# A decoder layer on one core: in the recurrence, a chunk's output products grouped by their contracted rows, and its norm in three parts

## The chip, the cores and the metric

The kernel runs on one core of one Trainium2 chip. A core has five engines that work side by side: PE (TensorE, matrix products), DVE (VectorE), ACT (ScalarE), POOL (GpSimd) and SP (SyncE, which here only issues transfers). Transfers between the chip's memory (HBM) and the core's memory (SBUF) are done by 16 DMA engines. PE writes its results into PSUM, eight banks of 128 partitions by 512 float32 values, from which DVE or ACT reads them.

The metric is the device time of one launch in microseconds. A profile is taken of one execution: it records when each instruction ran on each engine, which clock PE was granted, and what the transfers did. Its span is a little shorter than the time of that execution.

## What is computed

The reference is one decoder layer on 512 tokens of width 1024: a mixer block (an RWKV-7 recurrence beside a dilated attention, joined by gates) and then a PEER block (product-key experts). What matters here is the recurrence with its norm, for 16 heads of 64 channels:

```python
def step(state, inp):
    r_t, w_t, k_t, v_t, a_t, b_t = inp
    sa = jnp.einsum('bhij,bhj->bhi', state, a_t)
    state = (state * w_t[:, :, None, :] + sa[..., None] * b_t[:, :, None, :]
             + v_t[..., None] * k_t[:, :, None, :])
    return state, jnp.einsum('bhij,bhj->bhi', state, r_t)
...
y = wkv7_scan(r_h, hv(decay), k_h, v_h, -kk, kk * a_h)
mu = jnp.mean(y, axis=-1, keepdims=True)
var = jnp.mean(jnp.square(y - mu), axis=-1, keepdims=True)
y = (y - mu) * lax.rsqrt(var + RWKV_GN_EPS) * lnx_g.reshape(H, N) + lnx_b.reshape(H, N)
y = y + jnp.sum(r_h * k_h * r_k, axis=-1, keepdims=True) * v_h
return y.reshape(B, S, RWKV_WIDTH).astype(z.dtype) * g
```

The kernel doesn't take the 512 steps one by one. It cuts the sequence into NC = 8 chunks of C = 64 tokens, solves each chunk's own triangular system beforehand, and then hands a state of 64 x 64 values per head from chunk to chunk.

## The kernel before

`Kern.main` runs four phases one after the other: `phase_mod_n1` (modulation and the normed input n1), `phase_mix` (recurrence and attention), `phase_merge` and `phase_peer`. Large products are made by `gemm_ch`: it loads a weight tile of 512 KB (`wraw`, L124), splits it into a high part on ACT (`whi`, L127) and a low part on DVE (`wlo`, L128), and sums 24 products in one bank of PSUM (`ps_mm`, L141 to L143).

The order of the instructions on each engine is not that of the code. A planner (`schedule_with_timeline_sim`) lays them out along a timeline of its own, by priority and by what is ready; it also sets the waits between engines. The code's order gives the priority, and `first` raises that of the recurrence by AHEAD = 1500. On each engine the instructions then run in the order so fixed.

`attention` weaves two generators: `rw_chain`, three steps for each of the eight chunks, and `both()`, which makes the attention (`at_prep`, `at_core`, `at_end`) and between them gate columns by `gate_cols` (L403 and L404 store them). The gemms, transposes and softmax steps of attention thus fill PE between the steps of the recurrence.

A chunk c in `rw_chain` (L681 to L743), with the heads laid out as p = 0 to 7 and h = 0, 1 (h is the half of the 128 partitions):

- It loads `uv`, `ar`, `bks` and `mr` (512 KB each) from `pt_d` on SP: L694 to L700, in the trace `cuv`, `car`, `cbk` and `cmr`. The first three have two buffers, `cmr` has one.
- First step, for c > 0: `w0` (L705, in the trace `w`), 16 products of `ar` with the state `st`; then `w0s` on DVE (L708), two instructions.
- Second step: `up` (L715), 16 products with the solved system `tt`; its two halves are copied into `uv` by DVE (L716) and ACT (L717). Then one `next(norm, None)`, the first part of the norm of the chunk before.
- Third step: `sp` (L723), 16 products for the new state, added and scaled on DVE (L727, L728; L730 for c = 0); then `yp`, the chunk's output. For each of the 16 (p, h) there are two products into the same 64 x 64 place of one bank: the own one (L733), `mr` with `uv`, over all 128 rows, and the state's (L735), `ar` with `st`, over the 64 rows of half h. ACT copies `yp` to `ys` (L737).

`rw_norm` (L745 to L771) makes the norm of a chunk from `ys`. Its first part loads `bg` (`bgl`, one buffer, L749), and makes mean and difference on DVE (L751 to L753), the square on ACT (L755, tile `sqn`), the variance on DVE (L757, L758), its power -1/2 on POOL (L759) and the scaling on DVE (L760). Its second part turns the chunk by 16 products into `yt` (L766), multiplies it on DVE (L768, tile `yr`, which shares the one buffer of `sqn`), adds on POOL (L769) and stores to `yr_d` from SP (L770).

Before the change the generator of chunk c is made at the end of the chunk's loop body, its first part runs in chunk c+1's second step, and the second part when the loop comes to the end of chunk c+1's body (`run(norm)`, L741).

`yp` and `yt` both have tag "d", for which PSUM has one bank; `w0`, `up` and `sp` share tag "c", also one bank. After the eight chunks `phase_mix` reads `yr_d` back (`yrt`, L356) and splits it (L357, L358) for the gemms of `phase_merge`.

Of the kernel before, what the change touches and what calls it, by code (L numbers as in the profile page):

```python
# [77 lines left out]
def run(gen):  # L78
    for _ in gen:
        pass  # L80
# [20 lines left out]
class Kern:  # L101
# [579 lines left out]
    def rw_chain(self):  # L681

        nc, kp = self.nc, self.kp
        A = (slice(0, 64), slice(64, 128))
        PH = [(p, h) for p in range(8) for h in range(2)]
        st = None
        norm = iter(())
        def chain_ps(tag, name):
            return self.psum.tile([P, 8, C], F32, tag=tag, name=name, bufs=BANKS[tag])

        for c in range(NC):
            pt = self.pt_d[c]
            uv = kp.tile([P, 8, 128], F32, tag="cuv", name="cuv", bufs=2)
            nc.sync.dma_start(uv, pt[:, 3])  # L694
            ar = kp.tile([P, 8, 128], F32, tag="car", name="car", bufs=2)
            nc.sync.dma_start(ar, pt[:, 0])
            bks = kp.tile([P, 8, 128], F32, tag="cbk", name="cbk", bufs=2)
            nc.sync.dma_start(bks, pt[:, 2])
            mr = kp.tile([P, 8, 128], F32, tag="cmr", name="cmr")
            nc.sync.dma_start(mr, pt[:, 1])  # L700
            U = (slice(64, 128), slice(0, 64))
            if c:
                w0 = chain_ps("c", "w0")
                for p, h in PH:
                    nc.tensor.matmul(w0[A[h], p], ar[A[h], p, 0:64], st[A[h], p], start=True, stop=True)  # L705
                w0s = kp.tile([P, 8, C], F32, tag="w0s", name="w0s")
                for h in range(2):
                    nc.vector.tensor_tensor(w0s[A[h]], w0[A[h]], uv[A[h], :, U[h]], op=OP.add)  # L708
                ws = lambda p, h: w0s[A[h], p]
            else:  # L710
                ws = lambda p, h: uv[A[h], p, U[h]]
            yield
            up = chain_ps("c", "up")
            for p, h in PH:
                nc.tensor.matmul(up[A[h], p], self.tt[p // 4][A[h], (p % 4) * 8 + c, :], ws(p, h), start=True, stop=True)  # L715
            nc.vector.tensor_copy(uv[A[0], :, U[0]], up[A[0]])  # L716
            nc.scalar.activation(uv[A[1], :, U[1]], up[A[1]], AF.Copy)  # L717
            next(norm, None)
            yield
            if c < NC - 1:  # L720
                sp = chain_ps("c", "sp")
                for p, h in PH:
                    nc.tensor.matmul(sp[A[h], p], bks[:, p, h * 64:h * 64 + 64], uv[:, p, U[h]], start=True, stop=True)  # L723
                sn = kp.tile([P, 8, C], F32, tag="st", name="st", bufs=2)
                pc = self.pend[:, :, c:c + 1].to_broadcast([P, 8, C])
                if c:
                    nc.vector.tensor_tensor(sn, sp, st, op=OP.add)  # L727
                    nc.vector.tensor_tensor(sn, sn, pc, op=OP.mult)  # L728
                else:
                    nc.vector.tensor_tensor(sn, sp, pc, op=OP.mult)  # L730
            yp = chain_ps("d", "yp")
            for p, h in PH:
                nc.tensor.matmul(yp[A[h], p], mr[:, p, h * 64:h * 64 + 64], uv[:, p, U[h]], start=True, stop=not c)  # L733
                if c:
                    nc.tensor.matmul(yp[A[h], p], ar[A[h], p, 64:128], st[A[h], p], start=False, stop=True)  # L735
            ys = kp.tile([P, 8, C], F32, tag="ys", name="ys", bufs=3)
            nc.scalar.activation(ys, yp, AF.Copy)  # L737
            if c < NC - 1:
                st = sn
            yield  # L740
            run(norm)  # L741
            norm = self.rw_norm(c, ys)
        run(norm)  # L743

    def rw_norm(self, c, ys):  # L745

        nc, kp = self.nc, self.kp
        bg = kp.tile([P, 2, 8, C], F32, tag="bgl", name="bgl")
        nc.sync.dma_start(bg, self.bg_d[c])  # L749
        mean = kp.tile([P, 8], F32, tag="mean", name="mean", bufs=2)  # L750
        nc.vector.tensor_reduce(mean, ys, axis=AX.X, op=OP.add)  # L751
        nc.vector.tensor_scalar(mean, mean, 1.0 / 64, None, op0=OP.mult)
        nc.vector.tensor_tensor(ys, ys, mean[:, :, None].to_broadcast([P, 8, C]), op=OP.subtract)  # L753
        sq = kp.tile([P, 8, C], F32, tag="sqn", name="sqn")
        nc.scalar.activation(sq, ys, AF.Square)  # L755
        var = kp.tile([P, 8], F32, tag="var", name="var", bufs=2)
        nc.vector.tensor_reduce(var, sq, axis=AX.X, op=OP.add)  # L757
        nc.vector.tensor_scalar(var, var, 1.0 / 64, GN_EPS, op0=OP.mult, op1=OP.add)  # L758
        nc.gpsimd.tensor_tensor(var, var, self.hneg.to_broadcast([P, 8]), op=OP.pow)  # L759
        nc.vector.tensor_tensor(ys, ys, var[:, :, None].to_broadcast([P, 8, C]), op=OP.mult)  # L760
        yield

        yt = self.psum.tile([P, 8, C], F32, tag="d", name="yt", bufs=BANKS["d"])
        for p in range(8):
            for a in HALF:
                nc.tensor.matmul(yt[a, p], ys[a, p], self.ident[a, a], start=True, stop=True)  # L766
        yr = kp.tile([P, 8, C], F32, tag="sqn", name="yr")
        nc.vector.tensor_tensor(yr, yt, bg[:, 0], op=OP.mult)  # L768
        nc.gpsimd.tensor_tensor(yr, yr, bg[:, 1], op=OP.add)  # L769
        nc.sync.dma_start(self.yr_d[c], yr)  # L770
        yield  # L771
# [567 lines left out]
```

## Time and profile before

| | us |
|---|---|
| median of 3 runs | 2126.97 |
| lowest and highest | 2125.58 and 2130.1 |
| the profiled execution | 2125.92 |
| its span | 2124.1 |

Mean granted clock of PE over the profiled execution: 0.962 of full speed.

The profile's page gives, for each engine, the busy time in us, its share of the span and the number of instructions. Its slices cut the span into 40 equal parts; a digit is the busy share or the granted clock in tenths (9 is 90% or more). In the lists by line, a row names line, engine, operation, result and operands with their sizes; "x224" is a count, and three numbers with slashes are the shortest, median and longest duration in ns. In the timeline a row begins with its start and duration in us; rows that follow each other with the same text are merged with a count, and what stands in brackets is the engine's idle time before it and what ended it. A row of the list of waits names who waited for whom, then the total in us, the number of times and the longest.

PE shows twice: PEld is the loading of the stationary operand, PE the product itself. Products are pipelined: one may start before the one before it has ended, so the pace is read from start to start. "128\*64 128x64" is 128 contracted rows by 64 output columns of the stationary operand, and a moving operand of 64 columns.

### The profile page before, as it was taken

Reading aid. Unit: us, or ns where it says so; the run is one execution under the profiler, and the core shown is the slowest. Engines: PE = TensorE matmul, PEld = TensorE weight load, DVE = VectorE, ACT = ScalarE, POOL = GpSimd, SP = SyncE. Lnnn points to the kernel's source line nnn. Section 1 sums busy time; section 2 is a strip of 40 time slices with the busy share of each in tenths; the row PEclk is TensorE's granted clock in tenths of the full one; section 3 lists DMA queues with packets and bytes.
Section 4 is the critical chain, followed back from the end, with each engine's and each line's share of the span. In section 5 each row is a group of like instructions: output and inputs, shape, how many; then the busy total and the mean of one; then the engine's idle time right before and its main releaser. Section 6 shows DMA issues by size and latency. Waiting matters only on the chain.

```text
span 2124.1 us, 34025 instructions
## 1 busy us (share of the span) xinstructions
PE 2022.2 (95%) x12529; PEld 1744.0 (82%) x12529; DVE 1600.9 (75%) x3192; ACT 935.8 (44%) x1452; POOL 642.8 (30%) x511
## 2 busy tenths in 40 slices
PE   5999899999999998999999999999959999999999
PEld 4677667877877786899998999999958887877887
DVE  7466894853534555899999999987768898988555
ACT  3756665543324443334334454456633333333332
POOL 2424550221402111001674545420015555551000
PEclk9999989998889998999999999999979999999999
DMA  6666855354435532335998999985589999999763
GB/s 260 224 189 201 256 170 149 94 189 147 140 121 173 186 127 72 108 119 173 386 360 293 334 359 349 375 316 203 198 292 358 388 392 398 394 391 344 230 211 110
DMA packets 236299, 519.45 MB, mean 245 GB/s; under 512 B 35554, under 2 KB 129506, under 8 KB 233572
## 3 DMA queue, kind: packets, MB, share of 16 engines
q1 hardware_dynamic: 180260, 334.27, 46.4%
q0 software_dynamic: 36864, 134.23, 16.9%
q10 hardware_dynamic: 19008, 48.77, 6.0%
q8 instruction: 99, 1.62, 0.3%
q14 instruction: 68, 0.56, 0.1%
HBM read 432.23 MB, written 84.97 MB: 243 GB/s over the span
## 4 chain that ended last, share of the span: by engine, by line
PE 65%; DVE 16%; DMA 10%; issue 4%; ACT 3%; POOL 2%; SPq 0%; DVEq 0%; ACTq 0%; POOLq 0%
PE ps_mm L141 13%; PE ps_mm L143 13%; PE ps_mm L142 13%; DVE wlo L128 4%; PE gps L1132 4%; DMA wraw<-in_v 3%; DMA act<-act_d 2%; DVE row L1150 2%; PE yp L735 2%; PE yp L733 2%; PE ps_a L143 1%; PE ps_a L142 1%; PE ps_a L141 1%; DMA wada<-in_wada 1%; DVE acc L1164 1%
## 5 line engine op out<-in xcount | busy, mean ns | idle before, releaser
L127 ACT ACTIVATE whi<-wraw 128x1024 fp32r<-128x1024 f32 x356 | 370.1, 1042 | 388.6 <-PE ps_mm L142 226.9
L128 DVE TENSOR_TENSOR wlo<-wraw,whi 128x1024 fp32r<-128x1024 f32 x356 | 430.4, 1212 | 131.5 <-ACT whi L127 127.8
L141 PE MATMUL ps_mm<-n2h,whi 128*128 128x384 f32 (+1 forms) x1152 | 399.9, 347 | 3.2 <-ACT act L1203 3.2
L142 PE MATMUL ps_mm<-n2l,whi 128*128 128x384 f32 (+1 forms) x1152 | 398.2, 346 | 0.0
L143 PE MATMUL ps_mm<-n2h,wlo 128*128 128x384 f32 (+1 forms) x1152 | 396.1, 345 | 2.1 <-DVE wlo L128 2.1
L1141 POOL DMA_INDIRECT row<-in_v,xi x128 | 196.7, 1537 | 339.7 <-DVE acc L1164 166.5
L1141 POOL DMA_INDIRECT row<-in_u,xi x128 | 187.0, 1461 | 171.3 <-DVE dots L1150 132.7
L141 PEld LDWEIGHTS ps_mm<-n2h,whi 128*128 128x128 f32 x1152 | 218.4, 190 | 9.1 <-ACT act L1203 4.4
L143 PEld LDWEIGHTS ps_mm<-n2h,wlo 128*128 128x128 f32 x1152 | 218.2, 190 | 7.7 <-DVE wlo L128 2.8
L142 PEld LDWEIGHTS ps_mm<-n2l,whi 128*128 128x128 f32 x1152 | 218.3, 190 | 4.7
L141 PE MATMUL ps_mm<-n1h,whi 128*128 128x512 f32 x464 | 193.8, 421 | 8.8 <-ACT n1h L271 5.0
L143 PE MATMUL ps_mm<-n1h,wlo 128*128 128x512 f32 x464 | 192.5, 415 | 1.2 <-DVE wlo L128 1.2
L142 PE MATMUL ps_mm<-n1l,whi 128*128 128x512 f32 x464 | 192.4, 415 | 0.2 <-DVE n1l L272 0.2
L1250 ACT ACTIVATE wh<-act 128x384 fp32r<-128x384 f32 x128 | 66.9, 525 | 279.1 <-DVE act L1244 144.4
L1164 DVE SCALAR_TENSOR_TENSOR acc<-row,g,acc 128x1024 f32<-128x1024 f32 x127 | 162.3, 1278 | 0.8
L1150 DVE CUSTOM_DVE_ANT_0 row<-row,n2t 128x1024 f32<-128x1024 f32 x128 | 153.0, 1218 | 0.0
L1244 DVE TENSOR_TENSOR act<-act,G 128x384 f32<-128x384 f32 x128 | 69.8, 553 | 87.1 <-DMA act<-act_d 72.6
L1133 ACT ACTIVATE Gs<-gps 128x512 f32<-128x512 f32 x96 | 107.1, 1120 | 57.8 <-PE gps L1132 55.8
L141 PE MATMUL ps_mm<-whi,wh 128*128 128x512 f32 x256 | 92.6, 395 | 29.2 <-ACT wh L1250 29.0
L141 PEld LDWEIGHTS ps_mm<-n1h,whi 128*128 128x128 f32 x464 | 91.1, 198 | 32.5 <-ACT n1h L271 5.0
L143 PEld LDWEIGHTS ps_mm<-n1h,wlo 128*128 128x128 f32 x464 | 91.5, 197 | 23.0 <-DVE wlo L128 2.2
L142 PEld LDWEIGHTS ps_mm<-n1l,whi 128*128 128x128 f32 x464 | 92.1, 198 | 21.7 <-issue 2.4
(405 smaller groups left out, 4000.6 us busy)
## 6 DMA issues: line engine op xcount, KB each, us to landing
wraw<-in_uT SPq DMA_DIRECT2D x128, 512.0 KB
wraw<-in_v SPq DMA_DIRECT2D x128, 512.0 KB
wraw<-in_win SPq DMA_DIRECT2D x60, 512.0 KB
g_d<-Gs ACTq DMA_DIRECT2D x12, 2048.0 KB
G<-g_d SPq DMA_DIRECT2D x16, 1536.0 KB
act_d<-act ACTq DMA_DIRECT2D x120, 192.0 KB
act<-act_d SPq DMA_DIRECT2D x120, 192.0 KB
wada<-in_wada SPq DMA_DIRECT2D x64, 256.0 KB
```

The costliest lines, as they stand in the source:

```text
L127: nc.scalar.activation(hi[:, :n], raw[:, :n], AF.Copy)
L128: nc.vector.tensor_tensor(lo[:, :n], raw[:, :n], hi[:, :n].bitcast(F32), op=OP.subtract)
L141: mm(acc, lh, rh, start=start, stop=False)
L142: mm(acc, lh, rl, start=False, stop=False)
L143: mm(acc, ll, rh, start=False, stop=stop)
L1132: nc.tensor.matmul(g[:, j], E[:, j], A[:, j], start=True, stop=True)
L1133: nc.scalar.activation(Gs[:, :, o:o + 4].rearrange("p i t -> p t i"), g, AF.Copy)
L1141: self.nc.gpsimd.indirect_dma_start(row, None, self.I[tab], bass.IndirectOffsetOnAxis(ap=self.xi[:, n:n + 1], axis=0))
L1150: self.gathered(self.rowp, n, "u", lambda row: nc.vector.tensor_tensor_reduce(out=row, in0=row, in1=self.n2t, scale=1.0, scalar=0.0, op0=O ...
L1164: nc.vector.scalar_tensor_tensor(acc, row, self.gates0[:, n:n + 1], acc, op0=OP.mult, op1=OP.add)
L1244: nc.vector.tensor_tensor(act.rearrange("p (b t) -> p b t", t=GB), act.rearrange("p (b t) -> p b t", t=GB), G[:, :, n % GI, :], op=OP.mult)
L1250: nc.scalar.activation(wh, act, AF.Copy)
```

## The change

Three things are edited, all in `rw_chain` and `rw_norm`:

- The 32 output products of a chunk are issued in two groups: first the 16 of the state (64 contracted rows each), then the 16 own ones (128 rows). The mark `start`, which makes a product overwrite instead of add, is set on the first product of the bank alone (for each half h), no longer on the first product of each of the 16 places.
- `rw_norm` yields once more, after the square, so that it has three parts.
- The parts run at other places: the first (load of `bgl`, mean, difference, square) at the end of the chunk's own third step; the second (variance, power, scaling) in the next chunk's first step, behind `w0s`; the third (`yt`, `yr`, store) in the next chunk's second step, behind the copies of `up`.

```diff
@@ -706,6 +706,7 @@
                 w0s = kp.tile([P, 8, C], F32, tag="w0s", name="w0s")
                 for h in range(2):
                     nc.vector.tensor_tensor(w0s[A[h]], w0[A[h]], uv[A[h], :, U[h]], op=OP.add)
+                next(norm, None)
                 ws = lambda p, h: w0s[A[h], p]
             else:
                 ws = lambda p, h: uv[A[h], p, U[h]]
@@ -715,7 +716,7 @@
                 nc.tensor.matmul(up[A[h], p], self.tt[p // 4][A[h], (p % 4) * 8 + c, :], ws(p, h), start=True, stop=True)
             nc.vector.tensor_copy(uv[A[0], :, U[0]], up[A[0]])
             nc.scalar.activation(uv[A[1], :, U[1]], up[A[1]], AF.Copy)
-            next(norm, None)
+            run(norm)
             yield
             if c < NC - 1:
                 sp = chain_ps("c", "sp")
@@ -728,18 +729,21 @@
                     nc.vector.tensor_tensor(sn, sn, pc, op=OP.mult)
                 else:
                     nc.vector.tensor_tensor(sn, sp, pc, op=OP.mult)
+
             yp = chain_ps("d", "yp")
+            if c:
+                for p, h in PH:
+                    nc.tensor.matmul(yp[A[h], p], ar[A[h], p, 64:128], st[A[h], p], start=p == 0, stop=False)
             for p, h in PH:
-                nc.tensor.matmul(yp[A[h], p], mr[:, p, h * 64:h * 64 + 64], uv[:, p, U[h]], start=True, stop=not c)
-                if c:
-                    nc.tensor.matmul(yp[A[h], p], ar[A[h], p, 64:128], st[A[h], p], start=False, stop=True)
+                nc.tensor.matmul(yp[A[h], p], mr[:, p, h * 64:h * 64 + 64], uv[:, p, U[h]],
+                                 start=not c and p == 0, stop=p == 7)
             ys = kp.tile([P, 8, C], F32, tag="ys", name="ys", bufs=3)
             nc.scalar.activation(ys, yp, AF.Copy)
             if c < NC - 1:
                 st = sn
+            norm = self.rw_norm(c, ys)
+            next(norm)
             yield
-            run(norm)
-            norm = self.rw_norm(c, ys)
         run(norm)
 
     def rw_norm(self, c, ys):
@@ -753,6 +757,7 @@
         nc.vector.tensor_tensor(ys, ys, mean[:, :, None].to_broadcast([P, 8, C]), op=OP.subtract)
         sq = kp.tile([P, 8, C], F32, tag="sqn", name="sqn")
         nc.scalar.activation(sq, ys, AF.Square)
+        yield
         var = kp.tile([P, 8], F32, tag="var", name="var", bufs=2)
         nc.vector.tensor_reduce(var, sq, axis=AX.X, op=OP.add)
         nc.vector.tensor_scalar(var, var, 1.0 / 64, GN_EPS, op0=OP.mult, op1=OP.add)
```

## The prediction

> **What bounds the kernel now.** I read the page first: its busy times, then the granted clock in its 40 slices (one slice is 53.1 us).
>
> ```profile
> PE 2022.2 (95%) x12529; PEld 1744.0 (82%) x12529; DVE 1600.9 (75%) x3192; ACT 935.8 (44%) x1452; POOL 642.8 (30%) x511
> PEclk9999989998889998999999999999979999999999
> ```
>
> PE is busy for 95% of the span. The recurrence lies in slices 9 to 13, where the granted clock falls to 8. So I asked for the stretches of that stage and of those before and after it (busy us of PE, PEld, DVE, ACT, POOL, then granted clock, DMA share and GB/s).
>
> ```profile
> 100.00:300.00 200.00, 181.90 (x1265) 139.60 (x1264) 153.89 (x239) 125.22 (x232) 94.40 (x65) 0.90 0.72 216
> 300.00:440.00 140.00, 138.10 (x1347) 110.01 (x1347) 96.35 (x185) 84.44 (x170) 32.73 (x36) 1.00 0.43 131
> 440.00:672.00 232.00, 232.00 (x2154) 183.09 (x2156) 96.99 (x166) 77.35 (x194) 44.27 (x46) 0.86 0.42 139
> 672.00:700.00 28.00, 24.15 (x126) 18.66 (x124) 16.23 (x25) 15.78 (x27) 6.63 (x5) 0.94 0.83 287
> ```
>
> From 440 to 672 us PE has no idle time at all; DVE is busy for 42% of it, ACT for 33%, DMA for 42%. Whatever PE time goes here shortens the stage, as long as nothing else comes to the front. Next I looked at what PE does there, in the timeline of chunk 1 (start, duration, engine, line, operation, count).
>
> ```profile
> 468.54 0.39 PE L141 MATMUL ps_mm<-n1h,whi 128*128 128x512 f32 x1
> 468.86 0.33 PE L733 MATMUL yp<-cuv,cmr 128*64 128x64 f32 x2
> 469.12 0.33 PE L735 MATMUL yp<-st,car 64*64 64x64 f32 x2
> 469.37 1.15 PE L723 MATMUL sp<-cuv,cbk 128*64 128x64 f32 x32
> 470.36 0.28 PE L733 MATMUL yp<-cuv,cmr 128*64 128x64 f32 x2
> 470.57 0.33 PE L735 MATMUL yp<-st,car 64*64 64x64 f32 x2
> 470.83 0.33 PE L733 MATMUL yp<-cuv,cmr 128*64 128x64 f32 x2
> ...
> 479.35 0.47 PE L733 MATMUL yp<-cuv,cmr 128*64 128x64 f32 x2
> 479.76 0.47 PE L735 MATMUL yp<-st,car 64*64 64x64 f32 x2
> 480.16 1.11 PE L886 MATMUL ps_a<-ident,sc 128*128 128x128 f32 x4
> ```
>
> Every product of 64 columns shows as two passes. Where 16 products of one shape follow each other (sp, L723), 32 passes take about 1 us, 34 ns a pass from start to start. In yp, where L733 (128 contracted rows) and L735 (64 rows) alternate, two passes take 0.26 us at first (470.57 to 470.83) and 0.40 us at the end (479.35 to 479.76, 479.76 to 480.16). The step of 0.26 us holds 0.07 us of passes; about 0.19 us is spent at each change of the contracted rows. How much PE time that is in all, I took from a table of the seven stretches with yp's instructions alone (chunk 1 first, the sum last):
>
> ```profile
> 468.80:480.20 11.40, 10.42 (x64) 0.74 0.25 92
> sum 79.90, PE 69.68; mean PE 9.95
> ```
>
> So 64 passes of yp hold PE for 10.0 us a chunk, 69.7 us in chunks 1 to 7.
>
> **The change, part by part.**
>
> *Grouping the products.* The nearest rows of the new order are in chunk 0, where no state exists and nothing alternates, and in w (L705), which multiplies the same 64 rows of the state that L735 does:
>
> ```profile
> 452.86 1.15 PE L723 MATMUL sp<-cuv,cbk 128*64 128x64 f32 x32
> 453.84 0.99 PE L733 MATMUL yp<-cuv,cmr 128*64 128x64 f32 x28
> 455.34 1.15 PE L705 MATMUL w<-st,car 64*64 64x64 f32 x32
> 456.42 0.68 PE L894 MATMUL ps_a<-vt,ptr 128*64 128x64 f32 x14
> ```
>
> w's 32 passes hold PE from 455.34 to 456.42, 1.08 us; chunk 0's own products run at the same pace (28 in 0.99). Per later chunk the new yp is 1.08 us of state, 1.08 us of own products and one change between them, 0.2 us: 2.4 us, 17 us in seven chunks. Bounds: 2.16 us with no price for the change; 5.2 us if the planner cuts the groups some 16 times by other work (16 x 0.19 us = 3 us). I take 2.4, because the rows of w, up and sp stand in one piece. Gain: 69.7 - 17 = 53 us.
>
> One sum per bank (start on the first product only) adds and removes no instruction; nothing for it, since the gemm lines L141 to L143 add up in one bank at the pace of their neighbours. Bounds from below and above: the 34 ns of a pass, either way, 1 us in all.
>
> *The granted clock.* Behind each of the seven stretches there is a piece at half clock; first and last of seven, and their sum:
>
> ```profile
> 480.20:484.50 4.30, 4.30 (x61) 3.85 (x61) 1.55 (x3) 1.19 (x2) 0.00 (x0) 0.50 0.77 263
> 653.50:658.60 5.10, 5.10 (x31) 4.04 (x32) 2.38 (x6) 1.55 (x3) 0.00 (x0) 0.50 0.09 27
> sum 32.20, PE 32.20 PEld 27.50 DVE 13.97 ACT 11.64 POOL 0.61; mean PE 4.60 PEld 3.93 DVE 2.00 ACT 1.66 POOL 0.09
> 481.61 1.86 PE L705 MATMUL w<-st,car 64*64 64x64 f32 x29
> ```
>
> The same products of w take 1.86 us for 29 passes there and 1.15 us for 32 at full clock: 64 ns a pass against 36, a factor of 1.8. Without the slow clock these 32.2 us of work are 18, a gain of 14 us. It falls away only if the alternation causes the drop. For that speaks that in chunk 1 the drop begins inside the yp stretch (the step of two passes grows there from 0.26 to 0.40 us), that all seven pieces stand right behind one, and that 300 to 440 us, without yp, has 1.00; sp of chunk 0 and w behind it, grouped, run at 34 ns a pass. Bounds: nothing, or 15 us. I take 14.
>
> The Trainium skill, "TensorE: Matmul & The Clock Gate", Part 1 (The HAM clock gate), says that a busy TensorE is granted the full clock and that it drops to half after an idle window of about 3.4 us. By that rule alone the stretches, busy without a gap in the rows, would not drop, and their cause would have to be another, which stays; the sum by it would be 2077. The trace differs here: 0.74 granted in a stretch that is full of matmuls.
>
> *The norm in three parts.* It issues the same instructions in other places. Its first part (the load of bgl, mean, subtraction, square) goes from the next chunk's second step to the end of its own; variance to scaling goes behind w0s; the transposition yt and yr, which stood a chunk later still, go behind the copies of up, ahead of this chunk's sp and yp. On SP the load of bgl now stands ahead of the next chunk's loads of cuv, car, cbk and cmr. Its one buffer is free when POOL's L769 has added yr(c-1), which now comes before yp(c), so SP should not stand longer at it than before, and the weight loads (wraw) behind it neither. The loads of a chunk reuse buffers in a stage whose DMA share is 0.42 and would be 0.59 in the shortened one (0.42 x 232 / 165), below the 0.72 of 100 to 300 us. I take nothing; if SP did stand, PE would lack weights, at most the idle time bounded below. On DVE and ACT the work is the same, 97 and 77 us, in 165 us instead of 232: 59% and 47%, less than in 300 to 440 us (69% and 60%). On POOL 44 us in 165. One wait goes:
>
> ```profile
> ACT sqn L755 <- DMA yr_d<-yr: 9.4, 5, 2.4
> ACT ys L737 <- PE yp L735: 70.9, 7, 11.2
> ```
>
> The square shares its buffer with yr of the chunk before, whose store now leaves before yp; ACT's 9.4 us of standing may go. ACT is off the path: nothing.
>
> What gets a new wait is PE: yt and yp share the one bank of tag "d". Until now yp(c) came ahead of yt(c-1); now yp(c)'s first product waits until DVE has read yt(c-1) (L768), and behind it in PE's order stand yp itself and the gemms and transposes of attention. The chain that must be over by then, as durations:
>
> ```profile
> L753 DVE TENSOR_TENSOR ys<-ys,mean x8: 682/692/694, 456.5 to 655.0; 128x512 f32<-128x512 f32 x8
> L755 ACT ACTIVATE sqn<-ys x8: 620/632/634, 457.3 to 666.3; 128x512 f32<-128x512 f32 x8
> L759 POOL TENSOR_TENSOR var<-var,hneg x8: 1627/1645/2550, 459.6 to 667.9; 128x8 f32<-128x8 f32 x8
> 461.27 0.69 DVE L760 TENSOR_TENSOR ys<-ys,var 128x512 f32<-128x512 f32 x1 [1.81 <-POOL var L759]
> L768 DVE TENSOR_TENSOR yr<-yt,bgl x8: 691/691/694, 485.0 to 673.1; 128x512 f32<-128x512 f32 x8
> ```
>
> In chunk 0 the scaling ends at 461.96, 7.1 us behind the end of yp (454.83, 453.84 + 0.99); with yt (32 passes, 1.1) and yr (0.7) it makes 8.9 us. From one yp to the next PE will have 165 / 8, or 20 us, so this chain has about 9 us to spare. I take nothing, and as upper bound all 8.9 us a chunk.
>
> *What is late next.* Today PE's 10 us in yp hide every lateness of the other engines. With that cover gone, the recurrence itself (w, w0s, up, copies, sp, st) must fit into 20 us a chunk. Its DVE steps:
>
> ```profile
> 457.15 1.39 DVE L708 TENSOR_TENSOR w0s<-w,cuv 64x512 f32<-64x512 f32 x2
> 463.71 0.68 DVE L716 COPY cuv<-up 64x512 f32<-64x512 f32 x1 [0.61 <-PE up L715]
> 470.57 0.69 DVE L727 TENSOR_TENSOR st<-sp,st 128x512 f32<-128x512 f32 x1 [0.37 <-PE sp L723]
> 471.30 0.69 DVE L728 TENSOR_TENSOR st<-st,pend 128x512 f32<-128x512 f32 x1
> ```
>
> That is, at 1.08 us for each of three groups and 0.7 us for each of five DVE steps it is 7 us of work; I allow 10 with handovers (an estimate). Bounds for PE's new idle time: none, or the 9% that 100 to 300 us shows (18.1 of 200 us), 15 us of 165. The nearest row is 300 to 440 us, attention's gemms without yp: 1.9 of 140 us, 1.4%. That is 2 us; I take 4, because the recurrence makes PE wait at more places. In the tail (672 to 700, PE idle for 3.9 us) yr of the last chunk may come earlier; bounds 0 and 4 us gained, I take nothing, since attention's end stands there too.
>
> *Sum.* -53 - 14 + 4 = -63 us. The profiled execution took 2125.9 us (span 2124.1), 1.1 us below the median of 2127.0: 2125.9 - 63 = **2063 us**.
>
> **The rivals.**
>
> - *Other engines come to the front*: PE idle as in 100 to 300 us, 15 us. 2125.9 - 67 + 15 = 2074, up to 2080 if the idling costs clock as it does there (0.90). For it: the cover of 10 us a chunk goes. Against: DVE and ACT stay below their shares of 300 to 440 us, where PE is at 99%.
> - *The half clock stays*: it comes from something else than the alternation. Only the 53 us go, less 4: 2125.9 - 53 + 4 = 2077. For it: PE shows no idle time before the drops. Against: chunk 0. This is where the clock page's rule would put the time.
> - *The groups are cut*: the planner orders by its own timeline and already puts the first products of yp ahead of sp. If it sets other work, or own between state products, and half of the changes stay, half of 67 us goes: 2093.
> - *Slower*: PE stands in front of yp(c) until yr(c-1) has emptied bank "d". If none of the 8.9 us is covered, that is 62 us in seven chunks, and so long a stand may cost the 14 us of clock: 2125.9 - 53 + 62 = 2135. It decides from 53 / 7 = 7.6 us of standing a chunk. Against: other PE work lies before yp in its order, in chunk 1 the gemms between w and sp, some 11 us (up to 468.86):
>
> ```profile
> 457.44 0.48 PE L141 MATMUL ps_mm<-n1h,whi 128*128 128x512 f32 x1
> ```
>
> - *Nothing comes of it*: the price lies in adding a second product to a sum, not in the change of rows. Then 2126. Against: L141 to L143 add 24 times without such a price.
>
> **How the numbers follow.** Forecast 0.68; other engines 0.13; half clock stays 0.08; groups cut 0.06; slower 0.02; nothing 0.02; 0.01 for the rest, faster. Below the forecast: full gain 53 + 15 + 1, no idle time, 4 us of tail: 2053, and 3 us, chosen without a row, for a planner that orders the later program otherwise: 2050. Above: the cases of 2074 to 2080, and half clock with idle time, both losses together (53 us gained, 13 lost): 2086. Range 2050 to 2086. About 0.2% (4 us) is what a measurement of this kernel can tell from no change: faster by more 0.95, within 0.02, slower 0.03.
>
> **What would show it.** Right: the state's products stand as about 32 passes in a piece, the own ones too; yp holds PE for 2 to 3 us a chunk; the stage is some 63 us shorter and its granted clock near 1.00; ACT's wait for yp (10 us a chunk) is gone. Wrong: PE idle in the stage with DVE yr L768 or DVE st L727 as releaser (other engines, or bank "d"); pieces at 0.50 behind yp (clock); yp in pieces of two passes (cut). The time fails below if PE's idle time elsewhere shrinks, above if later stages give back what this one gains.

## The result, and the profile after

| | before | after |
|---|---|---|
| median of 4 runs | 2128.53 us | 2071.46 us |
| lowest and highest | 2125.58 and 2132.05 | 2069.71 and 2073.24 |
| profiled execution (span) | 2125.92 (2124.1) | 2073.24 (2071.4) |

After over before: 0.973, 95% interval 0.9717 to 0.9742. The changed kernel is 57 us faster; 2063 was forecast, from 2050 to 2086.

First the page of the changed kernel, its row of PE and its row of the granted clock.

```profile
PE 1959.7 (95%) x12529; PEld 1699.5 (82%) x12529; DVE 1606.0 (78%) x3192; ACT 938.4 (45%) x1454; POOL 639.8 (31%) x511
PEclk9999989999999989999999999999979999999999
```

PE runs the same 12529 instructions in 62.5 us less, and the run of digits 8 over the recurrence is gone. To see where the time went, the stage is cut alike in both kernels: from the first product of `up` (L715; L716 after) to DVE's first multiplication of a gate in the merge phase (L950; L955 after). Columns: window, its length, busy us of PE, PEld, DVE, ACT, POOL, granted clock, DMA share, GB/s. The view by windows, before:

```profile
444.00:712.10 268.10, 263.67 (x2303) 208.02 (x2303) 115.48 (x193) 97.67 (x228) 46.90 (x45) 0.87 0.46 151
```

and after, the stage as a whole and four pieces of 40 us of it:

```profile
443.90:652.90 209.00, 201.06 (x2304) 164.60 (x2304) 118.02 (x193) 100.17 (x230) 45.09 (x45) 0.98 0.58 198
440.00:480.00 40.00, 40.00 (x532) 33.13 (x530) 22.20 (x38) 17.15 (x41) 9.79 (x14) 1.00 0.67 230
480.00:520.00 40.00, 40.00 (x565) 33.17 (x560) 25.62 (x44) 21.14 (x48) 9.72 (x7) 1.00 0.59 198
520.00:560.00 40.00, 38.79 (x518) 31.96 (x517) 28.86 (x50) 16.46 (x46) 17.30 (x22) 1.00 0.61 204
560.00:600.00 40.00, 40.00 (x481) 32.52 (x480) 19.03 (x33) 17.38 (x48) 5.85 (x4) 1.00 0.43 147
```

The stage is 59.1 us shorter. PE is busy for 62.6 us less (263.67 to 201.06) and idle for 3.5 us more (268.10 - 263.67 = 4.4 before, 7.9 after). From 440 to 600 us PE is still all but full (158.79 of 160 us), now at a clock of 1.00.

How much of it yp is, from the same window of the view for yp's instructions alone; before, and then after:

```profile
460.00:660.00 200.00, 69.70 (x448) 0.84 0.40 128
```

```profile
460.00:660.00 200.00, 17.56 (x448) 0.97 0.59 202
```

The same 448 passes hold PE for 52.1 us less. What that looks like in chunk 1 and in chunk 4 shows the timeline of PE after (start, duration):

```profile
468.57 1.15 PE L724 MATMUL sp<-cuv,cbk 128*64 128x64 f32 x32
469.66 1.15 PE L736 MATMUL yp<-st,car 64*64 64x64 f32 x32
470.74 1.15 PE L738 MATMUL yp<-cuv,cmr 128*64 128x64 f32 x32
471.82 0.33 PE L891 MATMUL ps_a<-ident,sc 128*128 128x128 f32 x1
...
546.60 0.80 PE L738 MATMUL yp<-cuv,cmr 128*64 128x64 f32 x18
547.52 0.45 PE L705 MATMUL w<-st,car 64*64 64x64 f32 x8
547.90 0.33 PE L738 MATMUL yp<-cuv,cmr 128*64 128x64 f32 x2
548.16 0.32 PE L705 MATMUL w<-st,car 64*64 64x64 f32 x2
548.41 0.33 PE L738 MATMUL yp<-cuv,cmr 128*64 128x64 f32 x2
```

In chunk 1 each group stands as 32 passes in a piece, 1.08 us from start to start. In chunk 4 the planner lays the next chunk's `w` (64 rows) between yp's own products (128 rows), and the old step of 0.26 us for two passes is back. `w` goes into another bank than yp (tag "c", not "d"), so the step isn't the price of adding twice to one place.

PE's longest wait stands at the end of the stage. Its own waits in the whole stage, and then the chain of waits from 600 to 640 us (start, duration), both after:

```profile
PE ps_a L938 <- DVE ya L932: 5.4, 1, 5.4
PE w L705 <- issue: 1.1, 1, 1.1
PE ps_a L891 <- ACT sc L884: 1.0, 1, 1.0
```

```profile
614.48 5.12 DMA o_d<-ot
619.66 5.96 DMA oall<-o_d
...
627.43 4.63 DVE oall L930 x4
632.06 1.74 DVE ya L932 x2
633.85 1.54 PE ps_a L938 x6
```

No wait of PE for bank "d" is among them. The longest is attention's end: the store of its last block, the load of `oall`, and DVE's combination hold L938 until 633 us, and PE has run out of other work. The stage had idle time at its end before the change too: none from 440 to 672 us, so all of its 4.4 us behind that.

### The profile page after: what moved, and what is told of

It is laid out like the page before. It is cut to its first block, busy times and chain, and to the rows that moved or that the text cites. A ratio compares the mean times of both kernels' runs of the same rounds, so it can differ in the third digit from the quotient of the medians.

```text
span 2071.4 us, 34017 instructions
## 1 busy us (share of the span) xinstructions
PE 1959.7 (95%) x12529; PEld 1699.5 (82%) x12529; DVE 1606.0 (78%) x3192; ACT 938.4 (45%) x1454; POOL 639.8 (31%) x511
## 4 chain that ended last, share of the span: by engine, by line
PE 62%; DVE 17%; DMA 11%; issue 5%; ACT 3%; POOL 2%; SPq 0%; DVEq 0%; ACTq 0%; POOLq 0%
PE ps_mm L141 14%; PE ps_mm L143 13%; PE ps_mm L142 13%; DMA act<-act_d 4%; PE gps L1137 4%; DVE wlo L128 4%; DVE row L1155 2%; DMA wada<-in_wada 2%; PE ps_a L143 2%; PE ps_a L141 2%; PE ps_a L142 2%; DMA wraw<-in_v 2%; DVE acc L1169 1%; DMA G<-g_d 1%; POOL acc L443 1%
```

## The experiments

The twelve runs, of eleven variants and of the changed kernel once more, came in four groups, each beside runs of the kernel before on the same chip; medians of the kernel before were 2128.5, 2128.7, 2126.7 and 2128.5 us there.

**Grouping alone, norm in its old two parts at its old places.** The diff against the kernel before:

```diff
+            if c:
+                for p, h in PH:
+                    nc.tensor.matmul(yp[A[h], p], ar[A[h], p, 64:128], st[A[h], p], start=p == 0, stop=False)
             for p, h in PH:
-                nc.tensor.matmul(yp[A[h], p], mr[:, p, h * 64:h * 64 + 64], uv[:, p, U[h]], start=True, stop=not c)
-                if c:
-                    nc.tensor.matmul(yp[A[h], p], ar[A[h], p, 64:128], st[A[h], p], start=False, stop=True)
+                nc.tensor.matmul(yp[A[h], p], mr[:, p, h * 64:h * 64 + 64], uv[:, p, U[h]],
+                                 start=not c and p == 0, stop=p == 7)
```

> The products grouped (one sum per bank), the norm in two parts at its old places. Theory: the price lay in the changes between 128 and 64 contracted rows, so the grouping alone brings the gain: yp holds PE for some 17 us in chunks 1 to 7 instead of 69.7, no half clock behind it, time 2066 to 2080. Rival: the new places of the norm are needed for the gain (yr of the last chunk and the stores of yr earlier), then 2085 or more.

Measured: 2066.07 us (2063.71 to 2067.56), ratio 0.9708 (0.9681 to 0.9736); from 460 to 660 us yp holds PE for 18.23 us. The grouping brings 62 us, more than the whole change; its highest run lies below the lowest of the changed kernel.

**The norm's move alone**, the products alternating as before. The diff is that of the change without the lines of yp.

> The norm in three parts at its new places, the products alternating as before. Theory: yp still holds PE for about 69 us, PE stays without idle time in the stage, time 2122 to 2133, the same as before. Rival (the norm's places matter by themselves): 2115 or less.

Measured: 2132.70 us, ratio 1.002 (1.0001 to 1.0039): 4 us slower than before, by an interval that only just leaves out no change. In the profiled executions the stage is 5.6 us longer (273.7 and 268.1 us).

**One sum per bank alone**: the two products alternate as before, but `start` stands on the first product of the bank only.

```diff
-  mr[:, p, h * 64:h * 64 + 64], uv[:, p, U[h]], start=True, stop=not c)
+  mr[:, p, h * 64:h * 64 + 64], uv[:, p, U[h]], start=p == 0, stop=not c and p == 7)
...
-  ar[A[h], p, 64:128], st[A[h], p], start=False, stop=True)
+  ar[A[h], p, 64:128], st[A[h], p], start=False, stop=p == 7)
```

> As before, with the products alternating, but one sum per bank: the mark that makes a product overwrite stands on the first product of each half alone. Theory (changes of contracted rows): nothing moves, two passes still take 0.26 us at full clock, time 2124 to 2133. Rival (the price lies in opening and adding to 16 sums in one bank): yp falls to a few us a chunk and the time to 2070 to 2080.

Measured: 2129.68 us, ratio 1.0004 (0.9989 to 1.0018). The marks cost nothing and bring nothing. With the grouping's 62 us this also rules out that the price was in adding a second product, for the grouped kernel adds the same 16.

**Groups of two**: the changed kernel, with the state's products of p for both h and then the own ones of p, so that the rows change half as often as before the change.

```diff
+            for p in range(8):
+                if c:
+                    for h in range(2):
+                        nc.tensor.matmul(yp[A[h], p], ar[A[h], p, 64:128], st[A[h], p], start=p == 0, stop=False)
+                for h in range(2):
+                    nc.tensor.matmul(yp[A[h], p], mr[:, p, h * 64:h * 64 + 64], uv[:, p, U[h]],
+                                     start=not c and p == 0, stop=p == 7)
```

> The changed kernel, but with the products in groups of two instead of 16: two of the state, two own ones, and so on, which makes 15 changes of rows inside a chunk's yp instead of 1 (31 with alternation). Theory: at 0.19 us a change plus 64 passes of 34 ns yp takes 5.1 us a chunk, 19 us more in seven chunks than grouped by 16: about 2090. If stretches of 5 us also bring the half clock back, up to 14 us more: 2104. Rival (the price is per second product in a place, not per change): 2128.

Measured: 2081.45 us, ratio 0.9787 (0.9751 to 0.9823). The timeline of this kernel's PE in chunk 1:

```profile
475.68 0.33 PE L737 MATMUL yp<-st,car 64*64 64x64 f32 x4
475.94 0.34 PE L739 MATMUL yp<-cuv,cmr 128*64 128x64 f32 x4
476.21 0.33 PE L737 MATMUL yp<-st,car 64*64 64x64 f32 x4
476.47 0.34 PE L739 MATMUL yp<-cuv,cmr 128*64 128x64 f32 x4
```

A step of four passes takes 0.263 us, hardly more than the 0.257 us that the alternation needs for two. So a chunk's yp takes half of its time at full clock, 16 x 0.263 = 4.2 us, and the time stays below the 2090 us that I had expected from 0.19 us a change. And the clock stays full, in these windows of the same kernel:

```profile
480.00:520.00 40.00, 40.00 (x515) 31.88 (x515) 22.22 (x34) 16.82 (x40) 5.85 (x4) 1.00 0.60 189
560.00:600.00 40.00, 40.00 (x468) 32.39 (x468) 17.79 (x28) 13.75 (x33) 4.71 (x4) 1.00 0.59 185
```

The steps from the state's products to the own ones of the same place, and from those to the state's of the next place, take the same 0.26 us: the price goes with the change of rows, not with adding to the place just written.

After this group the question was why the changed kernel is 5 us behind the grouping alone.

**Four buffers for attention's output tile**, once in the changed kernel and once in the kernel with the grouping alone:

```diff
-  ax.tile([P, OW], F32, tag="ot", name="ot", bufs=2)
+  ax.tile([P, OW], F32, tag="ot", name="ot", bufs=4)
```

> The changed kernel with four buffers instead of two for attention's output tile ot. Theory A (the 5 us that the changed kernel is behind the kernel with the grouping alone lie in its tail: attention's last blocks stand at the store of ot, 4.6 us of DVE's waiting in two places, and attention's end comes late): 2067 to 2069 us. Rival B (they lie in the places of the norm, yt ahead of yp above all): 2071 us, as before, within 0.1%.

> The kernel before with the grouping alone and four buffers for ot. Theory A (store of ot in the tail): 2062 to 2064 us, 2 to 4 below the grouping alone (2066.1). Rival B: 2066 us.

Measured: 2068.89 us in the changed kernel, ratio 0.9725 (0.9706 to 0.9745). That is what theory A gave, but the interval overlaps that of the changed kernel. With the grouping alone 2060.38 us, 0.9687 (0.9667 to 0.9707), the lowest median of all; the interval overlaps that of the grouping alone. In the profiled executions the stage gets shorter by about the same in both, 209.0 to 203.2 us and 205.1 to 199.8. The waits that the buffers remove are these of the changed kernel, in DVE's timeline of attention's last four blocks (in brackets the idle time before and its releaser):

```profile
579.51 0.69 DVE L882 TENSOR_REDUCE ot<-sc 128x4 f32<-128x512 f32 x1
585.80 0.69 DVE L882 TENSOR_REDUCE ot<-sc 128x4 f32<-128x512 f32 x1
595.75 0.69 DVE L882 TENSOR_REDUCE ot<-sc 128x4 f32<-128x512 f32 x1 [2.02 <-DMA o_d<-ot]
604.02 0.69 DVE L882 TENSOR_REDUCE ot<-sc 128x4 f32<-128x512 f32 x1 [2.54 <-DMA o_d<-ot]
```

The kernel with the grouping alone shows no such wait and gains as much, so these waits are not all that the buffers change.

**Own products first**, then the state's, in the changed kernel; the two loops of yp change places.

> The changed kernel with the 16 own products ahead of the 16 of the state. In the changed kernel's chunk 4 the planner alternates the next chunk's w (64 rows) with the own products of yp (128 rows), 4.17 us in place of 2.23. With the own ones first, w can only meet the state's products, which have the same rows. Theory (each change of rows costs about 0.15 to 0.19 us): no stretch of yp above 2.5 us, and 2069 us, 2 to 3 us below the changed kernel. Rival (the planner puts it elsewhere, or the time given back is lost in the tail): 2071 us.

Measured: 2066.46 us, ratio 0.9713 (0.9692 to 0.9734): 5 us below the changed kernel, where 2 to 3 were expected. In the profiled executions the stage is 2.7 us shorter, as expected (206.3 and 209.0 us); the rest doesn't show there. In chunk 4 the planner still mixes w into yp, now as 64 rows among 64 rows, and in the timeline of this kernel's PE nothing is left of the step of 0.26 us:

```profile
547.84 0.22 PE L739 MATMUL yp<-st,car 64*64 64x64 f32 x1
547.87 0.22 PE L705 MATMUL w<-st,car 64*64 64x64 f32 x1
547.90 0.24 PE L739 MATMUL yp<-st,car 64*64 64x64 f32 x2
547.96 0.22 PE L705 MATMUL w<-st,car 64*64 64x64 f32 x1
```

yp holds PE for 16.2 us from 460 to 660 us, not 17.56.

**The norm's third part (yt, yr, store) back behind yp of the next chunk**; the first two stay at their new places:

```diff
-            run(norm)
             yield
...
             if c < NC - 1:
                 st = sn
+            run(norm)
             norm = self.rw_norm(c, ys)
             next(norm)
```

> The changed kernel with the norm's third part (yt, yr, store) back at its old place, behind yp of the next chunk; first and second part stay at their new places. Theory B (the norm's move costs 4 to 5 us because yt must have left bank d before yp can begin, so that yp and the work that follows it come later): 2066 us, as with the grouping alone. Rival (the price is in the first two parts, which DVE and ACT now run ahead of attention's work and of w0s): 2071 us.

Measured: 2061.94 us (2052.19 to 2067.24), ratio 0.9682 (0.9658 to 0.9706): some 10 us below the changed kernel, and below what either theory gave.

**The changed kernel again**, on the chip on which the last four ran:

> The changed kernel once more, on the same chip as the two runs beside it. If the distance between the changed kernel and its variants is real: 2070 to 2073 us. If it is the spread between chips: 2064 to 2067 us.

Measured: 2072.37 us (2070.26 to 2076.17), ratio 0.9746 (0.9733 to 0.976). The distance is real: none of its nine runs in both places is below 2069.7, none of the runs with the grouping alone, with yt back, or with grouping and four buffers above 2067.6. The stage repeats well: 209.0 and 209.1 us in the two profiles of the changed kernel. The rest of the span, whose code is the same in all the kernels, takes from 1853 to 1865 us in the profiles, so small differences are safer read from the stage.

**yt back and four buffers together**, then **yt alone moved**, in the kernel with the grouping: the whole norm runs in the next chunk's second step (`next(norm, None)` there becomes `run(norm)`).

> The norm's third part back behind yp of the next chunk (2061.9 us by itself), and four buffers for attention's output tile ot. If both act on the same thing (attention's last blocks and their stores come late), the buffers bring little more, for in the first profile DVE no longer waits for a store there: 2060 to 2062 us. If they act on different things, they add up (minus 9.5 and minus 2.6): 2058 to 2060 us.

> The grouping with the norm in two parts as before, but the second one (yt, yr, store) directly behind the first, in the next chunk's second step ahead of yp. Theory (the place of yt ahead of yp is what costs): 2071 us or more, 4 us or more above the grouping alone (2066.1), and attention's last store some 170 us behind the first up, not 160. Rival (the first two parts' places matter): 2066 us.

Measured: 2061.81 us, ratio 0.9699 (0.968 to 0.9719): the two don't add up. And 2064.73 us, 0.972 (0.9705 to 0.9736), where I had expected 2071 or more. **This one refutes the theory that yt ahead of yp is what costs.** Neither this move alone nor the earlier first two parts alone (the kernel with yt back) costs anything that can be seen; only both together do: the stage takes 202.4 us with yt alone moved and 198.9 with yt back, against 205.1 with the grouping alone and 209.0 in the changed kernel.

What they do to the stage shows when it is cut at attention's last block (ACT's copy of its output, L901, or L898 in the kernel with yt alone moved). Each fence has the stage up to there, and from there to the merge. The changed kernel, the kernel with yt back, and the kernel with yt alone moved:

```profile
443.90:614.00 170.10, 167.72 (x2164) 137.54 (x2163) 96.98 (x162) 75.61 (x191) 40.04 (x41) 0.99 0.56 189
614.00:652.90 38.90, 33.34 (x143) 27.07 (x142) 21.03 (x31) 24.56 (x39) 5.05 (x4) 0.91 0.68 234
```

```profile
449.80:608.70 158.90, 158.90 (x2121) 130.73 (x2121) 93.31 (x160) 74.27 (x190) 38.10 (x40) 1.00 0.59 194
608.70:648.70 40.00, 36.76 (x183) 29.36 (x183) 22.79 (x33) 22.86 (x39) 6.62 (x5) 0.96 0.76 260
```

```profile
443.80:608.50 164.70, 164.70 (x2122) 135.31 (x2122) 94.05 (x160) 74.59 (x191) 38.61 (x40) 1.00 0.57 184
608.50:646.20 37.70, 35.59 (x184) 28.07 (x183) 23.70 (x34) 22.08 (x37) 7.34 (x5) 1.00 0.78 268
```

What follows the last block takes about as long in all three, 38 to 40 us. But in the changed kernel that block comes 11 us later than with yt back (170.1 and 158.9 us into the stage), and more of PE's work is already done when it comes: 2164 instructions against 2121. So 143 instead of 183 are left to cover attention's end, PE is idle for 5.6 us there (38.90 - 33.34) and its clock falls to 0.91.

That reading, a late last block and so too little work to cover attention's end, doesn't hold for the 5 us between the grouping alone and the changed kernel. The grouping alone, cut in the same way:

```profile
446.00:605.20 159.20, 158.19 (x2140) 129.15 (x2139) 92.29 (x160) 72.70 (x188) 38.67 (x40) 1.00 0.59 190
605.20:651.10 45.90, 40.23 (x167) 32.27 (x165) 22.66 (x34) 24.30 (x40) 7.16 (x5) 0.93 0.66 228
```

Its last block comes as early as with yt back, and yet PE is idle for 5.7 us behind it, here in waits for the split of weights (3.47 us for `wlo`, 2.01 for `whi`). The same cut for all the kernels that bear on it, in us, with the last block's distance from the stage's start and the number of times that the contracted rows of PE's products change between 64 and 128 in the stage, counted in PE's timeline:

| kernel | stage | PE busy | PE idle | last block | changes of rows |
|---|---|---|---|---|---|
| before | 268.1 | 263.7 | 4.4 | 227.5 | 271 |
| changed | 209.0 | 201.1 | 7.9 | 170.2 | 87 |
| grouping alone | 205.1 | 198.4 | 6.7 | 159.3 | 49 |
| yt back | 198.9 | 195.7 | 3.2 | 159.0 | 46 |
| yt alone moved | 202.4 | 200.3 | 2.1 | 164.5 | 101 |
| own products first | 206.3 | 198.1 | 8.2 | 167.7 | 65 |
| changed, four buffers | 203.2 | 198.6 | 4.6 | 166.7 | 86 |
| grouping, four buffers | 199.8 | 195.7 | 4.1 | 158.2 | 48 |

From the grouping alone to the changed kernel the stage grows by 3.9 us: 2.6 of them are busy time of PE, 1.2 idle time. With four buffers in both it is 3.4 us, nearly all busy time (2.9). The rows change 38 times more in both pairs. So part of the norm's price may lie in the very thing that the grouping removes: with the norm at its new places the planner mixes products of 64 and of 128 rows again. Putting the own products first takes 22 of the changes away, and 3.0 us of busy time. The counts are a reading of the profiles, not an experiment, and they don't explain all: with yt alone moved there are 101 changes and the stage is still short.

**Attention's last core lifted in the planner's priority**, in the changed kernel, was to test the late last block as a cause:

```diff
-  parts = [(self.at_core(g), 8)]
+  parts = [(self.at_core(g) if g < 2 else self.first(self.at_core(g), 200), 8)]
...
-  def first(self, gen):
+  def first(self, gen, ahead=AHEAD):
```

(and `offset=ahead` in `first`).

> The changed kernel with the last of attention's three cores lifted in the planner's priority by 200, so that its four last blocks need not stand behind gate gemms. In the order that the planner lays down, 76 products of gemms then stand on PE between the last block and the first transposition of attention's end (L938), not 59. Theory (the norm's move costs its 5 us because too little work is left to cover attention's end: PE idle for 5.6 us of the last 38.9, at a mean clock of 0.91): 17 products of 0.25 us are 4 us more of cover, and the half clock behind the idle time shrinks: 2065 to 2068 us. Rival (the price is in the recurrence itself, in the 2 us of the mixed yp of chunk 4 and in other engines): 2071 us or more.

Measured: 2073.64 us, ratio 0.9742 (0.9724 to 0.976): nothing gained, a miss. The two windows of this kernel, cut in the same way:

```profile
446.30:617.60 171.30, 169.52 (x2170) 138.67 (x2169) 97.68 (x164) 76.72 (x193) 39.99 (x41) 1.00 0.58 190
617.60:658.90 41.30, 32.95 (x136) 26.08 (x135) 20.56 (x29) 23.49 (x37) 5.85 (x4) 0.88 0.62 211
```

and PE's idle time in the second of them, by its timeline:

```profile
635.95 0.80 PE L141 MATMUL ps_mm<-n1h,whi 128*128 128x512 f32 x1 [6.06 <-ACT whi L127]
640.41 0.80 PE L143 MATMUL ps_mm<-n1h,wlo 128*128 128x512 f32 x1 [2.29 <-DVE wlo L128]
```

The priority did not bring the last block forward (171.3 us into the stage), and the gemms that now stand before L938 wait for the split of their weights, 6.06 and 2.29 us. The edit did not make the condition that it was to test, so it shows nothing on the late last block. As the cause of the 5 us that block isn't shown, and the grouping alone speaks against it. Why the planner lays the blocks later and mixes the rows more when both parts are moved stays open.

## Why the prediction was right, and where it was not

- **What bounds the kernel**: right. PE stayed all but full through the recurrence (40.00, 40.00, 38.79 and 40.00 of four times 40 us), and its saved time became the kernel's.
- **Grouping, -53 us**: right; 69.70 to 17.56 us, -52.1. 2.4 us a chunk were forecast; in chunk 1 it is 2.2 (469.66 to 471.82, from start to start); the one cut group, in chunk 4, was foreseen as a rival that cuts them all. The price as I worded it, 0.19 us at each change, was wrong in form: added to four passes of 34 ns it makes 0.33 us a step, 5.2 us a chunk for groups of two; they took 0.263. The step is nearly the same for two passes and for four.
- **The clock, -14 us**: right in cause, too large. Without the alternation every window from 440 to 600 us has 1.00. Groups of two, with half as many steps, have 1.00 as well, so alternation as such doesn't bring the drop; whether it takes the longer stretch (10 us, not 4.2) or the shorter steps isn't separated. What PE's busy time lost beside yp is 62.6 - 52.1 = 10.5 us. The factor of 1.8 compared durations of merged rows, which run to the end of the last pass. From start to start the 29 passes of w take 1.56 us (481.61 to 483.17), 54 ns each against 34, a factor of 1.6: the 32.2 us become 20, a gain of 12. The rest fits two slow pieces that the changed kernel has, from 607.0 to 610.5 us (0.53) and from 633 to about 638 us.
- **One sum per bank, nothing**: right, ratio 1.0004 (0.9989 to 1.0018).
- **The norm in three parts: "I take nothing"**: this is the term that failed. By itself the move costs 4 us (2132.7 against 2128.5), and in the grouped kernel 5 (2071.5 against 2066.1; 3.9 us of the stage); with yt put back, it is 10 us better. The bound that I gave for it, PE standing up to 8.9 us a chunk in front of bank "d", looked at the wrong place: no such wait exists. I followed each moved instruction to what waits for it in the recurrence, and not to what the planner does with the work around it. In the grouped kernel it brought 38 changes of rows back and made PE's busy time 2.6 us longer, its idle time 1.2; how much of that the changes make isn't shown.
- **New idle time, +4 us**: right in size (3.5 us), and for the most part in place, though not in cause. Before, PE had no idle time up to the last block; after, it has 2.4 of 170.1 us there. Behind the block it was 4.4 us and is 5.6. But the waits there are for attention (L891, L938) and one for issue (L705), not for the recurrence's DVE steps.
- **Sum**: -63 was forecast, the stage gave -59.1 and the medians -57. Term by term the stage has -52.1 of grouping, -10.5 of clock and +3.5 of idle time, so the 3.9 us that are missing look like the clock's. The experiments show it otherwise: the grouping alone shortens the stage by 63.0 us and the time by 62, and the norm's move, put at 0, takes 3.9 to 5 back. That the grouping alone meets -63 so closely is in part luck: its terms are -65.3 of busy time, where -67 was forecast, and +2.3 of idle time, where it was +4. The range's upper end, 2086, rests on 13 us of loss for which the prediction shows no row; its own bound for idle time is 15.
- **The rivals**: "other engines come to the front" didn't come: ahead of attention's end ACT holds PE up once, for 1.0 us (L891), and DVE never; its 2074 is near the result, but for another reason. The half clock went, the groups held but for one, and the slower case's wait wasn't there.

## What to carry over

Where small products share PE, lay those of the same contracted rows side by side; count the changes of rows in the timeline, for the busy share hides them. When an edit gives a planner other priorities, its price is not in the moved instructions alone: look at what else moved, and count the same thing again. Time the parts of a change one by one: here one half of it brought more than the whole. And try an explanation on every kernel of the series: the late last block fitted three of them, and not the fourth.

## What the runs showed of the hardware

The price of changing rows isn't a sum of a fixed price and passes. Two passes between changes take 0.257 us a step, four take 0.263, and products that stay with 64 rows go through at some 30 ns a pass even where each changes its result and its slice of `car` (yp and w in turn, 547.84 to 547.96 above). Nor do other operands and another bank add anything: before the change, two passes of `ps_a` and two of yp, all with 128 rows, alternate from 643.84 to 644.10 us, 0.26 us for the four. The Trainium skill, "TensorEngine Tiling (Array Packing)", Key Properties, says that changing the tiling mode, not just the tile, drains TensorE. The trace agrees: tiles that alternate within 64 rows cost nothing, and between 64 and 128 rows each step costs a quarter of a microsecond; that the time goes into a drain, no run here shows.

The granted clock fell in stretches in which PE's rows leave no gap, 0.86 over 232 us before the change, and not where two passes more stood in each step. What the clock follows is thus not the busy time as the rows give it. In the changed kernel's tail it fell to 0.91 beside real idle time, which is how the Trainium skill, "TensorE: Matmul & The Clock Gate", Part 1, describes it; that rule alone would have left the stage before the change at full clock. Here PE stood for 5.4 us, and ran at 0.50 from 633.0 to 636.5 us; but the piece at half clock from 607.0 to 610.0 us came behind 1.0 us of idle time.
